# A two-layer decoder trunk: shared early chunks in the mixing's output projection, 512-wide last blocks before a row norm, and residual updates without GpSimd

## The chip, the cores and the metric

The kernel runs on one core of one Trainium2 chip. The metric is the device time of one execution in microseconds (us), as a median of several runs. The engines are named as the profile names them: PE is TensorE, DVE is VectorE, ACT is ScalarE, POOL is GpSimd and SP is SyncE, whose queue issues most of the DMAs.

## The reference

Two layers run over a residual stream of 256 positions and 2048 columns, all in float32. Each layer has three sub-layers, and each sub-layer is normalised before and after:

```python
for l in range(DEPTH):                                   # DEPTH = 2
    xn = rms_norm(h, mix_pre_g[l])
    proj = einsum('bsd,dc->bsc', xn, w_in[l])            # one projection for three head groups
    oa = diff_attention(...)      # 6 heads, 768 columns
    ob = dsa_attention(...)       # 6 heads, 768 columns, top-64 keys by an indexer
    oc = chunk_spatial_gating(gelu(cu), gelu(cv), ...)   # 512 columns
    mix = concatenate([oa, ob, oc], axis=-1)             # 2048 columns
    h = h + rms_norm(mix @ w_out[l], mix_post_g[l])
    xa = memory_attention(rms_norm(h, x_pre_g[l]), rms_norm(mem, mem_g[l]), ...)
    h = h + rms_norm(xa, x_post_g[l])
    ff = swiglu(rms_norm(h, f_pre_g[l]), f_w_gu[l], f_w_down[l])   # hidden width 5632
    h = h + rms_norm(ff, f_post_g[l])
```

`rms_norm(x, g)` divides each row by the root of its mean square and multiplies by `g`.

## The kernel before

**Matmuls and weights.** Every float32 operand is split into a high part `hi` (rounded to the engine's float32r) and a remainder `lo`, and a product is three matmuls: hi by hi, hi by lo, lo by hi. The weights come from memory as 1 MB pieces in three `raw` buffers. ACT makes `hi` (line 206) and DVE makes `lo` (line 207), for 1024 columns at a time, in three buffers each, so up to three split pieces are ready ahead of PE. `plan()` lists the order of all weight pieces. `weights()` hands them out: after each piece's matmuls are written it calls `prefetch` (the next split) and `pump`, which runs what is due (`later`) and lets each waiting generator (`start`) go one step. So the program order of everything beside the matmuls is set by how many weight pieces have gone by. A scheduler then orders each engine's queue by an estimated timeline, except where `ramp` keeps DVE and ACT in the written order.

`mm_t` keeps the weights stationary and streams 256 positions. `mm_n` keeps the 128x128 pieces of the activations stationary (two tiles `t`, positions 0 to 127 and 128 to 255) and streams up to 512 weight columns; with the contraction chunk `k` outside and `t` inside, there are six matmuls for a chunk. Accumulators are four PSUM buffers (`acc`), two for one `mm_n` block.

**The closing projections.** `project_out` (line 648) writes a sub-layer's output in blocks of columns, listed in `TAIL` (line 259): three of 512 and two of 256. It serves the mixing (16 chunks), the cross-attention (4 chunks) and the second half of the feed-forward part (22 chunks, `add=True`: the first half's result is added). After a block ACT squares it with a row sum (`square`, line 550), and it is multiplied by the post-norm gain `gb` into `og`, by DVE (line 673) or, with `add`, by POOL (line 669). The last block's product is put off into `rest` (lines 683 and 681).

**The mixing's first block.** Its 16 chunks come in the order 8 to 11, 0 to 3, 6 and 7, then 4 and 5, then 12 to 15 (`MIX_FIRST`, line 260). Chunks 4 and 5 are the last two heads of the differential attention and 12 to 15 are the gating; both are still computed by generators (`last_heads`, `gating`, `chunks`) while this block runs. The early chunks are read from buffers that the mixing's pool frees later (`early_place`).

**The residual step.** `residual` (line 579) takes the row sums, computes 1/rms (`row_rsqrt`, small DVE instructions at lines 467 to 475), adds `og` times that to the stream `H` (line 604), transposes the new `H` on PE (`turn_x`, line 564) and splits it into the next `x` (lines 212 and 213). After the mixing (`bare` false) the key projection of the memory (`t_k`, stationary weights, moving `mh` and `ml`) covers it, and columns 1024 to 2047 are added by ACT (line 601) and POOL (line 602). Elsewhere (`bare` true) nothing covers it but 38 dummy matmuls (`warm`). The very last step, `last_residual` (line 688), adds some pieces on PE (`hsum`) and the others on DVE, and stores the output.

Of the kernel before, what the change touches and what calls it, by code (L numbers as in the profile page):

```python
# [58 lines left out]
def trunk(ctx: ExitStack, tc, a, onehot, out):  # L59
# [17 lines left out]
    nc.gpsimd.memset(pc.tile([P, 8], F32, name="half_pc"), 0.0)  # L77
# [181 lines left out]
    TAIL = ((0, 512), (512, 512), (1024, 512), (1536, 256), (1792, 256))  # L259
    MIX_FIRST = ((8, 4), (0, 4), (6, 2), (4, 2), (12, 4))  # L260

    def plan():
# [7 lines left out]
        for l in range(L):  # L270
# [25 lines left out]
            for i, (c0, n) in enumerate(TAIL):  # L296
                yield spec(rows(w_out, c0, n), KD, n, MIX_FIRST if i == 0 else None)
# [7 lines left out]
            for hf in range(2):  # L305
# [3 lines left out]
                for c0, n in TAIL:  # L309
                    yield spec(rows(wd, c0, n), nh, n)  # L310
# [88 lines left out]
    def mm_n(nk, cols, xh, xl, hold=False):  # L399

        xh, xl = ([x[:, k, :] for k in range(nk)] if not isinstance(x, list) else x for x in (xh, xl))
        tiles = [acc.tile([P, 512], F32, tag="acc", name="acc") for _ in range(2)]
        for n, k, hi, lo in weights(nk, cols, hold):
            for t in range(2):
                o = tiles[t][:, :cols]
                h, lw = xh[k][:, t * P:(t + 1) * P], xl[k][:, t * P:(t + 1) * P]
                mm(o, h, hi, n == 0, False)
                mm(o, h, lo, False, False)
                mm(o, lw, hi, False, n == nk - 1)
        return tiles  # L410
# [174 lines left out]
    def residual(og, ss, evac, nxt, res, bare, off):  # L585
# [11 lines left out]
        def add(c, n, beside=False):  # L597
            f = slice(c * P, (c + n) * P)
            for t in range(2):
                if beside:  # L600
                    nc.scalar.activation(og[:, t, f], og[:, t, f], AF.Copy, scale=r[:, t:t + 1])
                    nc.gpsimd.tensor_tensor(H[:, t, f], H[:, t, f], og[:, t, f], op=ALU.add)
                else:
                    nc.vector.scalar_tensor_tensor(H[:, t, f], og[:, t, f], r[:, t:t + 1], H[:, t, f],  # L604
                                                   op0=ALU.mult, op1=ALU.add)
# [3 lines left out]


# [6 lines left out]
        if bare:  # L617
            prefetch()
# [6 lines left out]
        add(8, 4, not bare)  # L625
# [4 lines left out]
        add(12, 4, not bare)  # L630
# [17 lines left out]
    def project_out(nk, xh, xl, og, gain, add=False, first=None):  # L648
# [4 lines left out]
        for g, (c0, cols) in enumerate(TAIL):  # L653
# [6 lines left out]
            tiles = mm_n(nk, cols, *(first if first and g == 0 else (xh, xl)), hold=last)  # L660

            def evac(tiles=tiles, g=g, c0=c0, cols=cols, gb=gb, last=last):
# [626 lines left out]
```

## Time and profile before

| what | value |
|---|---|
| median of 3 runs | 2424.31 us (2423.04 to 2426.93) |
| time of the profiled execution | 2425.12 us |
| its span, first to last instruction | 2423.4 us |
| PE busy | 2389.2 us, 99% |
| DVE busy | 1412.6 us, 58% |
| ACT busy | 1188.7 us, 49% |
| POOL busy | 201.9 us, 8% |

Matmuls are pipelined, and the profile models their ends, so "busy" on PE means that one was under way and not that the array ran at its peak. How fast PE runs is better seen from the distance between the starts of neighbouring matmuls. Idle time on DVE, ACT and POOL costs nothing by itself.

### The profile page before, as it was taken

How to read it: one execution, taken by the hardware profiler on the slowest of the kernel's cores; microseconds unless marked ns; L12 is line 12 of the kernel's file. 1: busy time of each engine (PE TensorE's matmuls, PEld its weight loads, DVE VectorE, ACT ScalarE, POOL GpSimd, SP SyncE). 2: the span in 40 equal slices, each digit the busy share in tenths (PEclk: the TensorE clock that was granted, in tenths of full speed). 3: DMA queues.
4: the chain of work that ended last, by engine and by line, in shares of the span. 5: the costliest groups of instructions: out<-in, count | busy, mean ns of one | idle time of the engine just before them, and what ended most of it. 6: DMA issues, size and time to landing. Idle time of an engine off the chain costs nothing.

```text
span 2423.4 us, 42616 instructions
## 1 busy us (share of the span) xinstructions
PE 2389.2 (99%) x17741; PEld 2249.2 (93%) x17741; DVE 1412.6 (58%) x2129; ACT 1188.7 (49%) x1764; POOL 201.9 (8%) x177
## 2 busy tenths in 40 slices
PE   9999999999999999999999999999999999999998
PEld 8899789999998999998999997999999989999987
DVE  5686766665554455555466767666655544555554
ACT  5655545554444444444455655455544444444443
POOL 0010131000000000000100102100000000000001
PEclk9999999999999999999999999999999999999999
DMA  7755475455655565555554555644555555555553
GB/s 250 242 170 157 164 252 176 157 176 196 197 195 194 187 195 193 192 192 192 190 173 132 187 156 189 219 157 157 190 194 192 191 192 190 192 195 196 193 191 131
DMA packets 356757, 453.27 MB, mean 187 GB/s; under 512 B 11290, under 2 KB 275412, under 8 KB 356052
## 3 DMA queue, kind: packets, MB, share of 16 engines
q1 hardware_dynamic: 354836, 443.45, 55.9%
q0 software_dynamic: 1248, 6.29, 0.8%
q8 instruction: 139, 2.28, 0.4%
q10 hardware_dynamic: 480, 0.80, 0.1%
q14 instruction: 54, 0.44, 0.1%
HBM read 444.72 MB, written 5.79 MB: 186 GB/s over the span
## 4 chain that ended last, share of the span: by engine, by line
PE 91%; DVE 4%; ACT 2%; DMA 2%; issue 1%; SPq 0%; POOL 0%; ACTq 0%; POOLq 0%; DVEq 0%
PE acc L201 86%; DVE lo L207 2%; ACT hi L206 1%; PE xtp L564 1%; PE ixp L201 1%; ACT sqj L550 1%; PE lga L201 1%; DMA m<-in_mem_dram 1%; DVE H L604 1%; DMA H<-in_x_dram 0%; DVE mx L207 0%; PE warm L416 0%; DMA lp<-in_a_lambda_dram 0%; PE pvb L201 0%; PE lgx L201 0%
## 5 line engine op out<-in xcount | busy, mean ns | idle before, releaser
L207 DVE TENSOR_TENSOR lo<-raw,hi 128x1024 fp32r<-128x1024 f32 (+2 forms) x839 | 1000.9, 1194 | 870.7 <-ACT hi L206 868.4
L206 ACT ACTIVATE hi<-raw 128x1024 fp32r<-128x1024 f32 (+2 forms) x839 | 861.0, 1027 | 1037.7 <-PE acc L201 954.7
L201 PE MATMUL acc<-x,hi 128*128 128x256 f32 (+1 forms) x7360 | 1270.0, 277 | 0.0
L201 PEld LDWEIGHTS acc<-x,hi 128*128 128x128 f32 (+1 forms) x7360 | 1111.2, 188 | 2.8 <-issue 2.7
L201 PE MATMUL acc<-x,lo 128*128 128x256 f32 x3680 | 889.5, 278 | 6.8 <-DVE lo L207 4.6
L201 PEld LDWEIGHTS acc<-x,lo 128*128 128x128 f32 x3680 | 690.1, 188 | 13.4 <-DVE lo L207 6.1
L201 PE MATMUL acc<-hi,hx 128*128 128x512 f32 (+1 forms) x1760 | 452.6, 347 | 0.0
L201 PEld LDWEIGHTS acc<-hi,hx 128*128 128x128 f32 x1760 | 308.5, 189 | 41.7 <-issue 0.2
L201 PE MATMUL acc<-lo,hx 128*128 128x512 f32 (+1 forms) x880 | 304.9, 347 | 0.0
L201 PEld LDWEIGHTS acc<-lo,hx 128*128 128x128 f32 x880 | 166.7, 189 | 20.5 <-issue 0.2
L1243 POOL TENSOR_TENSOR g<-g,u 128x512 f32<-128x512 f32 x44 | 76.6, 1741 | 1131.3 <-ACT g L1241 1131.3
L201 PE MATMUL acc<-hi,mx 128*128 128x512 f32 (+1 forms) x576 | 148.1, 345 | 7.9 <-DVE mx L207 4.0
L201 PEld LDWEIGHTS acc<-hi,mx 128*128 128x128 f32 x576 | 99.6, 190 | 21.8 <-DVE mx L207 5.1
L201 PE MATMUL acc<-hi,x 128*128 128x384 f32 (+1 forms) x384 | 109.3, 360 | 0.0
L201 PE MATMUL acc<-lo,mx 128*128 128x512 f32 (+1 forms) x288 | 98.4, 343 | 0.1
L201 PEld LDWEIGHTS acc<-hi,x 128*128 128x128 f32 x384 | 70.1, 188 | 8.3 <-issue 3.3
L201 PE MATMUL acc<-lo,x 128*128 128x384 f32 (+1 forms) x192 | 69.7, 363 | 0.0
L212 ACT ACTIVATE x<-xtp,gT 128x256 fp32r<-128x256 f32 x96 | 39.5, 470 | 48.7 <-PE xtp L564 48.7
L201 PEld LDWEIGHTS acc<-lo,mx 128*128 128x128 f32 x288 | 54.6, 190 | 7.0 <-DVE lo L207 1.0
L213 DVE SCALAR_TENSOR_TENSOR x<-xtp,gT,x 128x256 fp32r<-128x256 f32 x96 | 41.6, 478 | 16.1 <-ACT x L212 15.9
L201 PE MATMUL acc<-hi,cx 128*128 128x512 f32 (+1 forms) x160 | 42.7, 352 | 0.0
L201 PEld LDWEIGHTS acc<-lo,x 128*128 128x128 f32 x192 | 36.1, 188 | 3.9 <-issue 1.3
(247 smaller groups left out, 1878.4 us busy)
## 6 DMA issues: line engine op xcount, KB each, us to landing
raw<-in_f_w_gu_dram SPq DMA_DIRECT2D x352, 512.0 KB, 4.5
raw<-in_f_w_down_dram SPq DMA_DIRECT2D x76, 1024.0 KB, 5.1
raw<-in_w_out_dram SPq DMA_DIRECT2D x30, 1024.0 KB, 5.4
raw<-in_w_in_dram SPq DMA_DIRECT2D x48, 512.0 KB, 4.7
raw<-in_w_in_dram SPq DMA_DIRECT2D x23, 1024.0 KB, 5.3
raw<-in_x_wkv_dram SPq DMA_DIRECT2D x16, 1024.0 KB, 4.9
raw<-in_w_in_dram SPq DMA_DIRECT2D x12, 960.0 KB, 5.1
raw<-in_x_wq_dram SPq DMA_DIRECT2D x8, 1024.0 KB, 5.2
```

The source lines that it names most:

```text
L201: return nc.tensor.matmul(o, lhsT=lhsT, rhs=rhs, start=start, stop=stop, skip_group_check=True)
L206: nc.scalar.activation(hi, src, AF.Copy)
L207: eng.tensor_tensor(lo, src, hi.bitcast(F32), op=ALU.subtract)
L212: nc.scalar.activation(hi, src, AF.Copy, scale=scale)
L213: nc.vector.scalar_tensor_tensor(lo, src, scale, hi.bitcast(F32), op0=ALU.mult, op1=ALU.subtract)
L550: nc.scalar.activation(q[:, :src.shape[-1]], src, AF.Square, accum_out=red)
L564: nc.tensor.transpose(p[:, t * P:(t + 1) * P], src[:, t, (c + j) * P:(c + j + 1) * P], ident)
L604: nc.vector.scalar_tensor_tensor(H[:, t, f], og[:, t, f], r[:, t:t + 1], H[:, t, f], op0=ALU.mult, op1=ALU.add)
L1243: nc.gpsimd.tensor_tensor(g, g, u, op=ALU.mult)
```

## The change

The mixing's first two blocks of 512 columns both run their ten early chunks first, into all four accumulators, and then their six late chunks. `TAIL` has four blocks of 512 wherever `project_out` is used; the first feed-forward half keeps the old widths (`HALF`). In a last block the final two chunks run for tile 0 first and then for tile 1, so that tile 0 is complete six matmuls earlier. The residual step after the mixing has an order of its own, two chunks a step, with all updates on DVE; the gain product of a last block is always on DVE. In `last_residual` 24 dummy matmuls are added, and the gain product comes later. Some padding tiles change, which moves the tile `cx` and the work pool by 64 bytes.

```diff
-    nc.gpsimd.memset(pc.tile([P, 8], F32, name="half_pc"), 0.0)
+    nc.gpsimd.memset(pc.tile([P, 24], F32, name="gap"), 0.0)
...
-    TAIL = ((0, 512), (512, 512), (1024, 512), (1536, 256), (1792, 256))
-    MIX_FIRST = ((8, 4), (0, 4), (6, 2), (4, 2), (12, 4))
+    TAIL = ((0, 512), (512, 512), (1024, 512), (1536, 512))
+    HALF = TAIL[:3] + ((1536, 256), (1792, 256))
+    MIX_EARLY, MIX_LATE = ((8, 4), (0, 4), (6, 2)), ((4, 2), (12, 4))
...
-            for i, (c0, n) in enumerate(TAIL):
-                yield spec(rows(w_out, c0, n), KD, n, MIX_FIRST if i == 0 else None)
+            for part, n in ((MIX_EARLY, 10), (MIX_LATE, 6)):
+                for c0, cols in TAIL[:2]:
+                    yield spec(rows(w_out, c0, cols), n, cols, part)
+            for c0, cols in TAIL[2:]:
+                yield spec(rows(w_out, c0, cols), KD, cols)
...
-                for c0, n in TAIL:
+                for c0, n in (HALF, TAIL)[hf]:
                     yield spec(rows(wd, c0, n), nh, n)
...
-    def mm_n(nk, cols, xh, xl, hold=False):
+    def mm_n(nk, cols, xh, xl, hold=False, into=None, more=False):
+        tiles = into or [acc.tile([P, 512], F32, tag="acc", name="acc") for _ in range(2)]
+        def step(t, n, k, hi, lo):
+            o = tiles[t][:, :cols]
+            h, lw = xh[k][:, t * P:(t + 1) * P], xl[k][:, t * P:(t + 1) * P]
+            mm(o, h, hi, n == 0 and not into, False)
+            mm(o, h, lo, False, False)
+            mm(o, lw, hi, False, n == nk - 1 and not more)
+        end = []
+        for w in weights(nk, cols, hold):
+            if hold and w[0] >= nk - 2:
+                end.append(w)
+                if w[0] < nk - 1:
+                    continue
+                for t in range(2):
+                    for w in end:
+                        step(t, *w)
+            else:
+                for t in range(2):
+                    step(t, *w)
...
-        def add(c, n, beside=False):
+        def add(c, n):
             f = slice(c * P, (c + n) * P)
             for t in range(2):
-                if beside:
-                    nc.scalar.activation(og[:, t, f], og[:, t, f], AF.Copy, scale=r[:, t:t + 1])
-                    nc.gpsimd.tensor_tensor(H[:, t, f], H[:, t, f], og[:, t, f], op=ALU.add)
-                else:
-                    nc.vector.scalar_tensor_tensor(H[:, t, f], og[:, t, f], r[:, t:t + 1], H[:, t, f],
-                                                   op0=ALU.mult, op1=ALU.add)
+                nc.vector.scalar_tensor_tensor(H[:, t, f], og[:, t, f], r[:, t:t + 1], H[:, t, f],
+                                               op0=ALU.mult, op1=ALU.add)
...
+        if not bare:
+            add(0, 2)
+            turn(0)
+            add(2, 2)
+            rest()
+            yield
+            turn(2)
+            for c in range(4, KD, 2):
+                add(c, 2)
+                yield
+                turn(c)
+            yield
+            yield from pre_norm(res)
+            return
...
-            tiles = mm_n(nk, cols, *(first if first and g == 0 else (xh, xl)), hold=last)
+            if g < len(early):
+                tiles = mm_n(6, cols, [xh[:, k, :] for k in range(KD)], [xl[:, k, :] for k in range(KD)], into=early[g])
+            else:
+                tiles = mm_n(nk, cols, xh, xl, hold=last)
             def evac(tiles=tiles, g=g, c0=c0, cols=cols, gb=gb, last=last):
+                def scaled(t, eng):
+                    d, p = og[:, t, c0:c0 + cols], tiles[t][:, :cols]
+                    if add:
+                        eng.tensor_tensor(d, d, gb, op=ALU.mult)
+                    else:
+                        nc.vector.tensor_tensor(d, p, gb, op=ALU.mult)
                 for t in range(2):
                     d, p = og[:, t, c0:c0 + cols], tiles[t][:, :cols]
                     if add:
                         nc.vector.tensor_tensor(d, p, d, op=ALU.add)
...
+                    square(d if add else p, ss[:, t, g:g + 1])
+                    if not last:
+                        scaled(t, nc.gpsimd)
+                return lambda: [scaled(t, nc.vector) for t in range(2)]
...
+        warm(24)
         dg = spread(r)
-        rest()
         for t, f in pieces[:3]:
             mm(summed[t, f.start], dg[:, t, :], og[:, t, f], False, True)
         for i in (3, 0, 4, 1, 5, 2, 6, 7):
             t, f = pieces[i]
+            if i == 2:
+                rest()
...
-        at = used[0]
+        at = used[0] + 1
...
+        early = [mm_n(10, cols, *first, more=True) for _, cols in TAIL[:2]]
+        oss, evac = project_out(KD, mxx[:, 0], mxx[:, 1], og, a["mix_post_g"][l], early=early)
...
-        cx = kp.tile([P, 2080], F32R, name="cx")[:, 32:].rearrange("p (a h t) -> p a h t", a=2, h=4)
+        cx = kp.tile([P, 2064], F32R, name="cx")[:, 16:].rearrange("p (a h t) -> p a h t", a=2, h=4)
```

## Rows read from the trace of the kernel before

**Rows 1.** The page: busy time by engine, and the chain that ended last.
```profile
PE 2389.2 (99%) x17741; PEld 2249.2 (93%) x17741; DVE 1412.6 (58%) x2129; ACT 1188.7 (49%) x1764; POOL 201.9 (8%) x177
...
PE 91%; DVE 4%; ACT 2%; DMA 2%; issue 1%; SPq 0%; POOL 0%; ACTq 0%; POOLq 0%; DVEq 0%
```

**Rows 2.** Windows: start:end, length, busy us (instructions) by engine, PE clock, DMA.
```profile
280.00:300.00 20.00, 15.68 (x74) 11.84 (x72) 14.56 (x39) 7.68 (x12) 6.83 (x6) 1.00 0.68 232
...
380.00:400.00 20.00, 17.32 (x138) 17.15 (x137) 16.59 (x24) 15.22 (x36) 5.67 (x4) 0.91 0.42 146
```

**Rows 3.** Waits of PE: total us, times, longest us.
```profile
PE acc L201 <- DVE lo L207: 10.0, 9, 2.7
PE acc L201 <- DVE mx L207: 4.0, 2, 2.0
PE acc L201 <- ACT mx L206: 3.9, 2, 1.9
```

**Rows 4.** Windows over the mixing's first block, and where the clock fell.
```profile
271.00:303.00 32.00, 27.67 (x131) 21.55 (x130) 23.56 (x51) 18.08 (x35) 6.97 (x6) 1.00 0.57 196
387.00:391.00 4.00, 3.77 (x19) 3.80 (x20) 3.92 (x7) 0.62 (x2) 0.00 (x0) 0.57 0.26 88
```

**Rows 5.** Groups of DVE instructions from 271 to 303 us.
```profile
L207 DVE TENSOR_TENSOR lo<-raw,hi 128x1024 fp32r<-128x1024 f32 x8 | 10.8, 1359 | 3.9 <-ACT hi L206 3.7
```

**Rows 6.** Timeline: start, length; H updates beside POOL, PE's wait; the last without POOL.
```profile
378.55 7.40 DVE L604 SCALAR_TENSOR_TENSOR H<-og,rs_r,H 128x256 f32<-128x256 f32 x8
...
379.94 5.73 POOL L602 TENSOR_TENSOR H<-H,og 128x512 f32<-128x512 f32 x4 [3.60 <-ACT og L601]
...
387.23 0.55 PE L201 MATMUL acc<-mh,lo 128*128 128x256 f32 x1 [2.68 <-DVE lo L207]
...
481.59 1.67 DVE L604 SCALAR_TENSOR_TENSOR H<-og,rs_r,H 128x256 f32<-128x256 f32 x4
```

**Rows 7.** Timeline of PE: first and last of four runs of matmuls.
```profile
1173.73 0.84 PE L201 MATMUL acc<-hi,hx 128*128 128x512 f32 x3
...
1178.94 0.39 PE L201 MATMUL acc<-lo,hx 128*128 128x512 f32 x1
...
1203.75 0.40 PE L201 MATMUL acc<-hi,hx 128*128 128x256 f32 x2
...
1210.59 0.40 PE L201 MATMUL acc<-hi,hx 128*128 128x256 f32 x2
...
468.79 0.39 PE L201 MATMUL acc<-lo,cx 128*128 128x512 f32 x1
...
472.29 0.39 PE L201 MATMUL acc<-lo,cx 128*128 128x512 f32 x1
...
473.00 0.39 PE L201 MATMUL acc<-hi,cx 128*128 128x256 f32 x2
...
474.02 0.50 PE L201 MATMUL acc<-hi,cx 128*128 128x256 f32 x3
```

**Rows 8.** Groups by form: count, busy us, mean ns of one.
```profile
L207 DVE TENSOR_TENSOR lo<-raw,hi 128x1024 fp32r<-128x1024 f32 x759 | 936.8, 1235 | 830.4 <-ACT hi L206 828.3
...
L213 DVE SCALAR_TENSOR_TENSOR x<-xtp,gT,x 128x256 fp32r<-128x256 f32 x96 | 41.6, 478 | 16.1 <-ACT x L212 15.9
...
L550 ACT ACTIVATE sqj<-acc 128x512 f32<-128x512 f32 x24 | 14.2, 590 | 14.0 <-PE acc L201 13.8
...
L673 DVE TENSOR_TENSOR og<-acc,gb 128x512 f32<-128x512 f32 x12 | 8.2, 683 | 1.4 <-ACT sqj L550 1.4
...
L550 ACT ACTIVATE sqj<-acc 128x256 f32<-128x256 f32 x16 | 6.1, 379 | 7.0 <-PE acc L201 7.0
```

**Rows 9.** Timeline of the kernel's end: DVE, PE and ACT.
```profile
2412.00 0.74 DVE L467 TENSOR_SCALAR rs_v<-ssr 128x2 f32<-128x2 f32 x1
...
2414.92 4.34 PE L201 MATMUL hsum<-og,dg 128*128 128x512 f32 x6 [2.68 <-DVE dg L487]
...
2419.30 0.60 ACT L706 ACTIVATE H<-hsum 128x512 f32<-128x512 f32 x1 [0.26 <-PE hsum L201]
```

More of the change, by code (lines that the diff above doesn't have):

```diff
@@ L397, in mm_t @@
         return tiles
-    def mm_n(nk, cols, xh, xl, hold=False):
+    def mm_n(nk, cols, xh, xl, hold=False, into=None, more=False):
         xh, xl = ([x[:, k, :] for k in range(nk)] if not isinstance(x, list) else x for x in (xh, xl))
[L402 to L409, printed above, removed]
+        tiles = into or [acc.tile([P, 512], F32, tag="acc", name="acc") for _ in range(2)]
[17 more added lines that the diff above has]
+                    step(t, *w)
         return tiles
@@ L616, in residual @@
         add(4, 2)
-        if bare:
-            prefetch()
+        prefetch()
         rest()
@@ L624, in residual @@
         turn(6)
-        add(8, 4, not bare)
+        add(8, 4)
         yield
@@ L629, in residual @@
         turn(10)
-        add(12, 4, not bare)
+        add(12, 4)
         yield
@@ L646, in begin, with project_out @@
         start(gen)
-    def project_out(nk, xh, xl, og, gain, add=False, first=None):
+    def project_out(nk, xh, xl, og, gain, add=False, early=()):
         ss = sm.tile([P, 2, len(TAIL)], F32, tag="sso", name="sso", bufs=2)
@@ L666, in evac @@
                         nc.vector.tensor_tensor(d, p, d, op=ALU.add)
-                        square(d, ss[:, t, g:g + 1])
-                        if not last:
-                            nc.gpsimd.tensor_tensor(d, d, gb, op=ALU.mult)
-                    else:
-                        square(p, ss[:, t, g:g + 1])
-                        if not last:
-                            nc.vector.tensor_tensor(d, p, gb, op=ALU.mult)
-                if not last:
-                    return
-                def rest():
-                    for t in range(2):
-                        d, p = og[:, t, c0:c0 + cols], tiles[t][:, :cols]
-                        if add:
-                            nc.gpsimd.tensor_tensor(d, d, gb, op=ALU.mult)
-                        else:
-                            nc.vector.tensor_tensor(d, p, gb, op=ALU.mult)
-                return rest
+                    square(d if add else p, ss[:, t, g:g + 1])
+                    if not last:
+                        scaled(t, nc.gpsimd)
+                return lambda: [scaled(t, nc.vector) for t in range(2)]
             if last:
@@ L1120, in trunk @@
         pool = {}
-        at = used[0]
+        at = used[0] + 1
         def turn_memory():
-            while used[0] == at or any(g.__name__ in ("last_heads", "chunks") for g in side):
+            while used[0] <= at or any(g.__name__ in ("last_heads", "chunks") for g in side):
                 yield
@@ L1132, in trunk @@
         start(turn_memory())
-        oss, evac = project_out(KD, mxx[:, 0], mxx[:, 1], og, a["mix_post_g"][l], first=first)
+        early = [mm_n(10, cols, *first, more=True) for _, cols in TAIL[:2]]
+        oss, evac = project_out(KD, mxx[:, 0], mxx[:, 1], og, a["mix_post_g"][l], early=early)
         kp = pool["kp"]
@@ L1250, in trunk @@
             if hf == 0:
-                for c0, cols in TAIL:
+                for c0, cols in HALF:
                     t_d = mm_n(nh, cols, hh, hl)
```

## The prediction

> **What bounds the kernel now.** I read the page first. PE is busy for 2389 of 2423 us, and the chain that ended last is PE's for 91% [rows 1]: time can only come from PE's remaining waits, from slow matmuls, or from the ends where nothing follows. I then cut the span into windows of 20 us. The feed-forward windows are full. The dents in each layer are the mixing's closing (15.68 of 20 us busy) and the stretch after it, where the next key projection runs beside the residual step: 17.32 busy, at a mean clock of 0.91 [rows 2]. Layer 1 repeats both with nearly the same numbers. PE's waits say what ends them: twice 2.0 us for DVE's and twice 1.9 us for ACT's split of a late mixing chunk, and 2.7 us for a weight split, the longest of nine [rows 3]. Last I compared starts of neighbouring matmuls, form by form, since "busy" hides their rate.
>
> The reader is to see two different illnesses. In the closing, DVE is busy for only 23.56 of 32 us while PE waits [rows 4]: the data are late because their chain is long, and matmuls that could run are queued behind those that cannot. In the key projection DVE is the late engine itself. Eight updates of `H` take 7.40 us beside four POOL additions of 5.73 us together, where four without POOL take 1.67 [rows 6]; so eight should take 3.34, and 4.06 us are lost. The weight split queues behind them, PE waits 2.68 us [rows 6], and then the clock is at half: 0.57 over 387 to 391 [rows 4].
>
> **The change part by part.** The sum is made against the profiled execution, 2425.12 us.
>
> *Shared early chunks.* The second block's ten early chunks now stand where PE waited: 60 matmuls of 0.2265 us (from 1173.73 to 1178.94 there are 23 starts [rows 7]), 13.6 us more cover. Chunks 4 and 5 arrived 2 us late and 12 to 15 about 2 us late behind them, so 13.6 us covers both, unless DVE falls behind. Over the twenty early chunks (27.2 us of PE) it has ten weight splits of 1.235 us [rows 8], 12.4 us, and what it does now beside splits, 23.56 less 10.8 [rows 4, 5], 12.8 us: 25.2 in all. Tight, but four of the eight chunk splits are wanted only by the third block. Now 7.9 us are lost over both layers [rows 3]; I leave 0.4 a layer: **-7.1** (bounds -7.9 and 0). The second block now reads 60 of its matmuls from early copies, whose address may suit PE less; by the slower 512-wide row, 0.2333 [rows 7], that is 0.4 us a layer at most: **+0.4** (0 to 0.8). The accumulators: block one and two hold all four until block one's late chunks end. Its emptying (two squares of 0.59, two products of 0.683 [rows 8]) hides under block two's 36 late matmuls, 8.2 us; without that cover it would cost 2.5. Loads keep their bytes; one more is issued on SP. `turn_memory` starts after 20 chunks and not 16, some 60 us before the key projection needs it: nothing. POOL issues four gain loads and not five.
>
> *Updates without ACT and POOL.* DVE now does sixteen updates of 0.42 (1.67/4 [rows 6]), 6.7 us; sixteen chunk splits of 0.478 [rows 8], 7.6; two gain products of 0.683, 1.4; the 1/rms chain, 2.9 (2412.00 to 2414.92 [rows 9], an upper value); eight weight splits, 9.9. That is 28.5 us against a key projection of 192 narrow matmuls at 0.1133 (473.00 to 474.02 is nine [rows 7]), 21.8 us, plus PE's own transposes. The surplus runs into the query projection, which wants a further chunk only every 12 x 0.1133 = 1.36 us. What matters is order: updates now come two chunks at a time, so a weight split stands behind some 1.8 us of DVE work and not behind 7.40, and up to two split pieces are ready beyond the one in use. Nothing else queues on POOL here. Gone would be the waits (2.7 a layer) and the half clock: 4 us at 0.57 is 1.7 us, of which some is the wait itself, so 1.5. I leave 0.5 a layer: **-7.4** (bounds -8.4 and 0).
>
> *Blocks of 512.* In the mixing and the feed-forward part a pair of 256-wide matmuls takes 0.240 us (1203.75 to 1210.59 is 57 starts) and one of 512 takes 0.2265 [rows 7]. Pairs that go: 16 x 6 = 96 and 22 x 6 = 132 a layer, 456 in all, at 13.5 ns: -6.2. In the cross-attention it is the other way: 0.2333 for 512 and 0.1133 for 256 [rows 7], so 48 pairs cost +0.3, unless the 64 bytes by which `cx` moves change its rate; at 0.2265 throughout it would be -1.0. Together **-5.9** (-7.2 to -5.9).
>
> The Trainium skill, "TensorE: Matmul & The Clock Gate", section "Back-to-back issue gap", gives the distance of warm matmuls as columns / 2.4 + 2.5 ns. By it one of 512 saves only 2.6 ns over two of 256, and this term would be an estimated -1.3. I go by the rows, since block three beside the narrow ones has the same operands.
>
> *Three row norms with only dummy matmuls as cover.* The wide last block makes the square 0.59 long and not 0.38 [rows 8], and the sum before it longer alike. But tile 0 is complete six matmuls, 1.36 us, earlier, so its share is done when tile 1 ends. Two gain products on DVE, 1.4 us, enter the ramp, where DVE has gaps while it waits for PE's transposes; uncovered they would delay the next split by 1.4. POOL no longer stands beside the chain (a 0.17 us instruction took 0.74 beside it at the end [rows 9]). I take **0** (-0.6 to +0.7 each).
>
> *The end.* The 24 dummies fill PE's 2.68 us wait, so the six `hsum` matmuls (4.34 us, partly at half clock [rows 9]) may run at full clock, about 1.5 us sooner. Then DVE ends last: five 0.68 us pieces from 2414.69 end at 2418.1, and two products more make 2419.5, against 2419.90 for the last ACT copy. The chain loses the 0.57 us beside POOL. **-0.9** (-1.8 to 0).
>
> Sum: -7.1 + 0.4 - 7.4 - 5.9 + 0 - 0.9 = -20.9; 2425.12 - 20.9 = 2404.2. The profiled execution is 0.8 above the median of the three runs, so **2403.4** as a median.
>
> **The rivals.**
>
> *The key projection keeps its wait.* DVE's 28.5 us exceed PE's time there, and the scheduler may still put updates and chunk splits in a row. For: it did so before, eight in a row. Against: 4.06 us of those were POOL's doing. Price: the 7.4 come back, 2411.
>
> *The closing still waits.* Twenty early chunks load DVE to 25.2 of 27.2 us, so the late chunks may come later than they do now. For half of the wait to stay costs 3.6: 2407.
>
> *The width buys nothing.* The narrow rate may belong to where `hi` and `lo` lie and not to the width; `cx` shows the opposite order [rows 7]. If one of 512 saves only a tenth or two of the 13.5 ns, the term falls to about -1: 2408.
>
> By the formula of the Trainium skill ("TensorE: Matmul & The Clock Gate", "Back-to-back issue gap") it would also be an estimated 2408.
>
> *Moved tiles.* If the padding doesn't keep the addresses of the mixing's and feed-forward pools, 7 x 132 wide matmuls a layer may run at 0.2333: 1848 x 6.8 ns = 12.6 us, and 528 narrow ones gain 3.5: 2412.
>
> *The other side: DVE serves its own work before the weight splits, in closing and key projection.* Now it does so once a layer. At the extreme all 12.8 us in the closing and all 18.6 (28.5 - 9.9) in the key projection go first; less the 5.4 us that two ready pieces cover (24 matmuls), PE waits 7.4 and 13.2 us, each with 1.5 for the clock. Over what I leave, that is 22.6 a layer, 45.2 in all: 2449. It decides the sign once more than 57% of it happens (25.8 us to reach 2429.2); at three quarters the time is 2437. Against it: splits are written ahead of each step, and they were slipped into the 1/rms chain before.
>
> **How the numbers follow.** The forecast's case, with its bounds (2397 to 2407), has 0.60; the key projection's wait 0.14; the closing's 0.08; the width 0.05; moved tiles 0.05; the slow side 0.04; better than 2397 0.04. Low end: nearly all waits and the end's whole 1.8 us, 2395. High end: both waits kept in part, 2414. A measurement of this kernel tells about 0.2%, 4.8 us, from no change. All cases but the slow one end faster by more than that; with some weight for two of them together, and for a schedule that moves work elsewhere, faster is 0.90, same 0.05, slower 0.05. The likeliest time is 2403.
>
> **What would show it.** Right: no wait for `mx` on PE between the gating projection and the third block; starts 0.2265 apart in all four blocks; no half clock after the mixing; updates of 0.42 us each in pairs, no POOL beside them; `hsum` at full clock. Wrong: a wait for `lo` over 2 us in the key projection, with the clock at half after it; PE waiting for a transpose whose update is late; the third block waiting for an accumulator; a last block at 0.233. The prediction fails as a whole if DVE is more than 90% busy over both stretches and PE waits there for its weight splits.

## The result, and the profile after

The kernel after takes 2398.47 us (median of 4 runs, 2397.03 to 2399.35), the kernel before 2424.39 beside it: a ratio of 0.9891, 95% interval 0.9874 to 0.9908. The forecast was 2403 us, with a range of 2395 to 2414. The profiled execution is the one of 2399.35 us, 25.8 below that of before. The page of after, busy time by engine and the chain that ended last (before: [rows 1]):

```profile
PE 2379.1 (99%) x17261; PEld 2224.6 (93%) x17261; DVE 1406.9 (59%) x2131; ACT 1183.4 (49%) x1726; POOL 184.0 (8%) x159
...
PE 95%; ACT 2%; DVE 2%; DMA 1%; issue 0%; SPq 0%; POOL 0%; ACTq 0%; POOLq 0%; DVEq 0%
```

PE is the chain even more than before. The largest sum among its waits (total us, times, longest; before: [rows 3]), and the windows over the closing's early part and over the key projection, with busy us of each engine and then the clock (before: [rows 2, 4]):

```profile
PE acc L201 <- DVE lo L207: 4.3, 7, 0.8
```

```profile
272.00:300.00 28.00, 28.00 (x133) 23.26 (x132) 21.22 (x48) 18.02 (x34) 3.98 (x2) 1.00 0.53 170
366.00:391.00 25.00, 25.00 (x217) 24.94 (x216) 23.59 (x61) 18.58 (x38) 0.54 (x1) 1.00 0.49 180
```

No wait for `mx` is left, and none for `lo` over 0.8 us. Both dents are full, at full clock: 28.00 of 28.00 and 25.00 of 25.00 us. DVE is at 94% in the second (23.59 of 25.00 us), so it has little to spare there.

Where the time went is read from starts of matmuls in PE's timeline, stretch by stretch. This table is worked out from them (us; layer 0, layer 1; the last column is after less before, both layers):

| stretch | before | after | change | forecast |
|---|---|---|---|---|
| start of the span to the closing of layer 0 | 271.26 | 272.20 | +0.9 | 0 |
| closing, first matmul on an early copy to the mixing's last | 101.14, 97.17 | 93.81, 90.46 | -14.0 | -9.3 |
| from there to the query projection's first | 29.50, 29.46 | 25.14, 25.14 | -8.7 | -7.4 |
| cross-attention's closing | 23.86, 23.86 | 23.31, 23.31 | -1.1 | +0.3 |
| second feed-forward closing | 121.33, 122.17 | 119.47, 121.24 | -2.8 | -3.6 |
| three row norms with dummies, in order of time | 5.74, 7.08, 5.74 | 5.85, 6.29, 5.85 | -0.6 | 0 |
| last closing matmul to the span's end | 13.15 | 13.52 | +0.4 | -0.9 |

The sum is -25.9, against -25.7 by the spans; the rest of the kernel is as it was. (The forecast's -2.6 and -3.6 for the width stand in the lines where the pairs are.) The first line is no part of the change: over all kernels below the closing of layer 0 starts between 270.6 and 274.6 us after the span's start, and PE's wait for the first pieces of `x`, 0.2 to 2.8 us, varies with it. So spans are compared from there on.

### The profile page after: what moved, and what is told of

The parts are those of the page before. It is cut to its first block, busy times and chain, and to the rows that moved or that the text cites. A ratio compares the mean times of both kernels' runs of the same rounds, so it can differ in the third digit from the quotient of the medians.

```text
span 2397.7 us, 41589 instructions
## 1 busy us (share of the span) xinstructions
PE 2379.1 (99%) x17261; PEld 2224.6 (93%) x17261; DVE 1406.9 (59%) x2131; ACT 1183.4 (49%) x1726; POOL 184.0 (8%) x159
## 3 DMA queue, kind: packets, MB, share of 16 engines
q0 software_dynamic: 1216, 6.29, 0.8%
## 4 chain that ended last, share of the span: by engine, by line
PE 95%; ACT 2%; DVE 2%; DMA 1%; issue 0%; SPq 0%; POOL 0%; ACTq 0%; POOLq 0%; DVEq 0%
PE acc L201 89%; PE xtp L584 1%; DVE lo L207 1%; PE ixp L201 1%; ACT sqj L570 1%; ACT hi L206 1%; PE lga L201 1%; PE warm L436 1%; DMA m<-in_mem_dram 1%; PE pva L201 0%; PE pvb L201 0%; PE ptp L444 0%; PE lgx L201 0%; PE pvx L201 0%; ACT x L212 0%
## 5 line engine op out<-in xcount | busy, mean ns | idle before, releaser
L207 DVE TENSOR_TENSOR lo<-raw,hi 128x1024 fp32r<-128x1024 f32 (+3 forms) x833 | 1000.9, 1203 | 869.0 <-ACT hi L206 866.7
L206 ACT ACTIVATE hi<-raw 128x1024 fp32r<-128x1024 f32 (+3 forms) x833 | 859.9, 1033 | 1026.9 <-PE acc L201 947.2
L201 PEld LDWEIGHTS acc<-hi,hx 128*128 128x128 f32 x1584 | 286.4, 189 | 48.4 <-issue 0.2
L201 PEld LDWEIGHTS acc<-lo,hx 128*128 128x128 f32 x792 | 149.4, 189 | 23.9 <-issue 0.2
L201 PE MATMUL acc<-hi,mx 128*128 128x512 f32 x384 | 120.7, 391 | 0.0
L201 PEld LDWEIGHTS acc<-hi,mx 128*128 128x128 f32 x384 | 71.9, 188 | 14.8 <-DVE mx L207 0.2
L201 PE MATMUL acc<-lo,mx 128*128 128x512 f32 x192 | 75.0, 391 | 0.0
L201 PEld LDWEIGHTS acc<-lo,mx 128*128 128x128 f32 x192 | 36.1, 188 | 7.4
L201 PE MATMUL acc<-hi,m 128*128 128x512 f32 x128 | 41.8, 398 | 0.0
L201 PE MATMUL acc<-hi,cx 128*128 128x512 f32 x128 | 41.2, 395 | 0.0
```

Source lines behind the costliest of these rows:

```text
L201: return nc.tensor.matmul(o, lhsT=lhsT, rhs=rhs, start=start, stop=stop, skip_group_check=True)
L206: nc.scalar.activation(hi, src, AF.Copy)
L207: eng.tensor_tensor(lo, src, hi.bitcast(F32), op=ALU.subtract)
```

## The experiments

**The shared early chunks alone**, on the kernel before:

```
-            tiles = mm_n(nk, cols, *(first if first and g == 0 else (xh, xl)), hold=last)
+            if g < len(early):
+                tiles = mm_n(6, cols, ..., into=early[g])
...
+        early = [mm_n(10, cols, *first, more=True) for _, cols in TAIL[:2]]
```

> The kernel before with the shared early chunks alone (five blocks, updates with ACT and POOL as before). Cover theory: the waits and short gaps of the closing go by the longer cover alone; from the first matmul that reads an early copy to the last of the mixing it took 101.1 us in layer 0 and 97.2 in layer 1 before, and 93.8 and 90.5 after with 1.3 of that from the width. So about 95.1 and 91.8 here, the key projection as before with its wait and its half clock, and about 2413 us in all. Rival, the term as I priced it (6.7 us for both layers): 96.8 and 93.8... and 2417.5. Rival, the cover works only together with the other two parts, or the key projection pays it back: over 2420.

Measured: 2414.07 us, ratio 0.9944 (0.9930 to 0.9958). Its closing takes 95.95 and 91.88 us, 5.2 and 5.3 less than before: 10.5 in all. Windows of it, closing and key projection:

```profile
275.00:303.00 28.00, 28.00 (x136) 23.34 (x135) 21.52 (x49) 17.68 (x32) 3.98 (x2) 1.00 0.51 169
371.00:400.00 29.00, 26.30 (x216) 26.12 (x216) 24.45 (x49) 20.50 (x44) 6.29 (x5) 0.94 0.46 155
```

The closing's window is full without the other two parts. The key projection keeps its 2.7 us wait in both layers; the lower clock comes behind it in layer 0 alone (29.6 us at a mean of 0.94; 28.1 us in layer 1, at 1.00). The cover works by itself, and is worth half as much again as I had priced it.

**A shorter cover**: the kernel after, with four early chunks of the second block in place of ten.

```
-            for part, n in ((MIX_EARLY, 10), (MIX_LATE, 6)):
+            for part in (MIX_EARLY, MIX_EARLY[:1], MIX_LATE, MIX_EARLY[1:] + MIX_LATE):
...
-        early = [mm_n(10, cols, *first, more=True) for _, cols in TAIL[:2]]
+        early = [mm_n(n, cols, *first, more=True) for n, (_, cols) in zip((10, 4), TAIL[:2])]
```

> The kernel after with only four of the second block's chunks early and not ten: 14 early chunks, 24 matmuls or 5.4 us of cover more than before, and not 60 or 13.6. Threshold theory: what was late came about 2 us late twice, so 5.4 us is nearly enough: the closing within 1 us of the kernel after in each layer (93.8 and 90.5), 2398.5 to 2400.5 in all. Rival, it is DVE's sum of work and the gain grows with the cover: 40% of it, some 3 us a layer lost again, 2404 to 2405.

Measured: 2403.98 us, ratio 0.9908 (0.9894 to 0.9921). The closing takes 97.63 and 92.59 us, 3.8 and 2.1 more than in the kernel after. So four chunks of ten give some 4.5 of the 10.5 us (10.5 less 5.95), and my threshold theory, which left at most 1 us a layer, falls. That the gain grows evenly with the cover isn't shown either: what is lost is one wait a layer, and in layer 0 the clock behind it. PE waits for a weight split that took 2.07 us where one takes 1.235 [rows 8], and POOL multiplies beside it (timeline of POOL, DVE and PE, in brackets the idle time ahead and what ended it; then windows of the 4 us from the wait on, layer 0 and layer 1, the clock third from the end):

```profile
296.95 3.49 POOL L1117 TENSOR_TENSOR MX<-MX,y 128x512 f32<-128x512 f32 x2 [5.58 <-DVE y L1115]
...
297.24 2.07 DVE L207 TENSOR_TENSOR lo<-raw,hi 128x1024 fp32r<-128x1024 f32 x1
...
299.37 0.76 PE L201 MATMUL acc<-lo,mx 128*128 128x512 f32 x1 [1.52 <-DVE lo L207]
```

```profile
299.00:303.00 4.00, 3.63 (x9) 2.88 (x10) 2.68 (x3) 0.63 (x1) 2.09 (x3) 0.57 0.98 321
1491.00:1495.00 4.00, 3.79 (x17) 3.14 (x18) 3.02 (x4) 1.69 (x2) 3.67 (x5) 1.00 0.97 355
```

The wait is 1.52 us in both layers; at the clock of 0.57 layer 0 loses an estimated 1.7 us more (4 us times 0.43), which is the difference between 3.8 and 2.1.

**The updates: POOL or order?** Four kernels have the update step in four mixtures. First, the kernel before with all updates on DVE, in its old order of four chunks at a time:

```
-        add(8, 4, not bare)
+        add(8, 4)
...
-        add(12, 4, not bare)
+        add(12, 4)
```

> The kernel before, its sixteen residual updates after the mixing all on DVE, still written four chunks at a time. Engine theory (POOL and ACT beside DVE made the updates long): the stretch from the last matmul of the mixing to the first of the query projection falls from 29.5 to about 25.1 us in both layers, no half clock there, about 2415.7 us in all. Order theory (what counts is that weight splits are not queued behind a long row of updates, as my prediction had it): eight updates of 0.42 us still stand together, some 3.3 us, and four more than before are DVE's; the stretch stays over 27.5 us and the whole over 2420.

Then the kernel after, with ACT and POOL back for columns from 1024 on, in the new order:

```
         def add(c, n):
             f = slice(c * P, (c + n) * P)
             for t in range(2):
+                if c >= 8 and not bare:
+                    nc.scalar.activation(og[:, t, f], og[:, t, f], AF.Copy, scale=r[:, t:t + 1])
+                    nc.gpsimd.tensor_tensor(H[:, t, f], H[:, t, f], og[:, t, f], op=ALU.add)
+                else:
```

> The kernel after, with ACT's scaling and POOL's addition back for columns from 1024 on after the mixing, written two chunks at a time as in the new order. Engine theory: updates beside POOL are twice as long again, the stretch from the last matmul of the mixing to the query projection goes back to 28 to 29.5 us, with a wait for a weight split of about 2 us; 2405 to 2407 us. Order theory: the new order keeps the splits ahead, the stretch stays at 25 to 26 us; 2398 to 2400.

Then the kernel after with the old step whole:

```
-            for c in range(4, KD, 2):
-                add(c, 2)
-                yield
-                turn(c)
...
+        add(8, 4, not bare)
...
+        add(12, 4, not bare)
```

> The kernel after with the whole residual step of before after the mixing: four chunks at a time, columns from 1024 on by ACT and POOL in pieces of 512. With the updates on DVE alone the wait went in the old order too, and with POOL in the new order most of it went as well (25.1 to 26.5 us for the stretch from the last matmul of the mixing to the first of the query projection, in place of 29.5). If the two are remedies of one wait, either of them enough, here with neither the stretch is 29 to 29.5 us again and the whole about 2406. Rival: other parts of the change (wide last block, earlier memory) already shortened it, and the updates count little: 26 to 27 us, 2401.

Measured: 2416.26 us (0.9957, 0.9944 to 0.9969) for the first; 2401.46 (0.9895, 0.9881 to 0.9908) for the second; 2407.11 (0.9922, 0.9908 to 0.9936) for the third. From the mixing's last matmul to the query projection they take 24.99 and 24.75 us; 26.53 and 26.49; 29.82 and 28.18. So POOL's absence is enough in the old order, the new step recovers most with POOL in place, and with neither the wait is back, 2.4 us long (with the lower clock behind it in layer 0 alone, as above). Neither of my two theories alone predicts all three. What goes with the wait in all of them is how long DVE's row of updates lasts before its next weight split. Timeline rows of it (start, length, count): after; the first; the second (with POOL's row); the third.

```profile
372.16 4.44 DVE L620 SCALAR_TENSOR_TENSOR H<-og,rs_r,H 128x256 f32<-128x256 f32 x11
```

```profile
381.16 3.26 DVE L604 SCALAR_TENSOR_TENSOR H<-og,rs_r,H 128x256 f32<-128x256 f32 x8
```

```profile
371.70 5.22 DVE L624 SCALAR_TENSOR_TENSOR H<-og,rs_r,H 128x256 f32<-128x256 f32 x8
...
373.18 8.41 POOL L622 TENSOR_TENSOR H<-H,og 128x256 f32<-128x256 f32 x8 [4.82 <-ACT og L621]
...
376.85 3.44 DVE L207 TENSOR_TENSOR lo<-raw,hi 128x1024 fp32r<-128x1024 f32 x2
```

```profile
372.54 6.42 DVE L624 SCALAR_TENSOR_TENSOR H<-og,rs_r,H 128x256 f32<-128x256 f32 x8
...
374.24 5.86 POOL L622 TENSOR_TENSOR H<-H,og 128x512 f32<-128x512 f32 x4 [5.03 <-ACT og L621]
...
381.32 0.50 PE L201 MATMUL acc<-mh,lo 128*128 128x256 f32 x1 [2.38 <-DVE lo L207]
```

Rows of 3.26 and 4.44 us leave PE no wait; 5.22, with two slow splits behind, leaves 0.7, 6.42 leaves 2.4, and the 7.40 of before [rows 6] 2.7. POOL works through the length of one update (0.65 to 0.93 us beside it as a mean of the row, 0.41 without), and of the splits too (1.72 beside it, 1.235 without). It is POOL and not ACT: in the kernel after, updates with ACT at work through most of their time take 0.48 us each, as the others do. The second and the third mixture differ in one more thing than order: POOL adds in pieces of 256 columns in the second and of 512 in the third. An update that lies wholly beside such an addition takes 0.97 us in the second and 1.5 in the third and before. So how much of what the second recovers is due to the order, and how much to POOL's shorter pieces, isn't shown. The updates do not come two chunks at a time in any kernel; the scheduler puts 8 or 11 in a row, and 15 in the next kernel.

**Five closing blocks again**, in the kernel after:

```
-    TAIL = ((0, 512), (512, 512), (1024, 512), (1536, 512))
-    HALF = TAIL[:3] + ((1536, 256), (1792, 256))
+    TAIL = ((0, 512), (512, 512), (1024, 512), (1536, 256), (1792, 256))
+    HALF = TAIL
```

> The kernel after with five closing blocks again (the last two of 256 columns) in mixing, cross-attention and both feed-forward halves; padding set so that the later tiles lie as in the kernel after. Width theory: 96 and 132 pairs of matmuls a layer at 13.5 ns are 6.2 us, those of the cross-attention nothing (0.2265 for 512, 0.1133 for 256 with cx where it lies now); the row norm's ramps change by up to 0.8 each: 2404.5 us (2403 to 2406). Rival, the gain came with the moved tiles and not with the width: within 1 us of the kernel after, 2398 to 2400.

Measured: 2406.22 us, ratio 0.9912 (0.9898 to 0.9925), a span 6.4 longer: +3.6 in the two mixing closings, +2.8 in the two feed-forward ones, +0.8 in the cross-attention, +1.1 over key and query projection (here 15 updates stand in a row, 6.03 us, with waits of 0.7), -1.0 at the end. That is just above my range. In the mixing's +3.6 a wait of 0.7 for the memory's DMA in layer 0 is contained, which the kernel after doesn't have. So in the mixing and the feed-forward part the width is worth about what the rows of before said, and the scheduler's row of updates hangs on it as well. In the cross-attention I had the narrow rate wrong. Two rows of its 256-wide closing matmuls, 45 starts apart:

```profile
464.02 0.28 PE L201 MATMUL acc<-lo,cx 128*128 128x256 f32 x1
...
469.42 0.28 PE L201 MATMUL acc<-lo,cx 128*128 128x256 f32 x1
```

That is 0.120 us a matmul (5.40 over 45) where `cx` lies now, and it was 0.1133 where it lay before [rows 7].

**cx where it lay before:**

```
-        cx = kp.tile([P, 2064], F32R, name="cx")[:, 16:]...
+        cx = kp.tile([P, 2080], F32R, name="cx")[:, 32:]...
```

> The kernel after with cx 64 bytes further, where it lay before. Address theory: its 512-wide matmuls start 0.2333 us apart again and not 0.227, the cross-attention's closing is 23.9 us and not 23.3, in both layers. Rival, the rate came with the width: 0.227 and 23.3 as in the kernel after.

Measured (one run, 2402.59 us), from PE's timeline: 23.88 us in both layers, about as before (23.86), against 23.31 in the kernel after. Two rows of it near the closing's end, five matmuls apart, and two of the kernel after, nine apart:

```profile
468.68 0.39 PE L201 MATMUL acc<-hi,cx 128*128 128x512 f32 x1
...
469.85 0.40 PE L201 MATMUL acc<-hi,cx 128*128 128x512 f32 x1
```

```profile
464.82 0.39 PE L201 MATMUL acc<-lo,cx 128*128 128x512 f32 x1
...
466.86 0.40 PE L201 MATMUL acc<-hi,cx 128*128 128x512 f32 x1
```

That is 0.234 us a matmul here (1.17 over five) and 0.227 there (2.04 over nine), at one width. The 64 bytes made that rate. They move the two widths in opposite ways: 0.2333 and 0.1133 for 512 and 256 columns at the old place, 0.227 and 0.120 at the new one, and there `cx` has the rates of `hx` (0.2265 and 0.120 [rows 7]). So one matmul of 512 saves some 13 ns over two of 256 at the new place, and costs 6.7 more than two at the old one: what a wide block is worth hangs on where the activations lie.

**Four blocks in the first feed-forward half too:**

```
-    HALF = TAIL[:3] + ((1536, 256), (1792, 256))
+    HALF = TAIL
```

> The kernel after with four closing blocks of 512 in the first feed-forward half too. In layer 0 the second half's closing went from 121.3 to 119.5 us by it, so 1.8 us a layer: 3.6 us, about 2395. Rival, the first half has no row norm behind it but ACT's evacuation and the next gating matmuls that wait for the accumulators: what is won waits there, 2398.

Measured: 2414.12 us, ratio 0.9949 (0.9936 to 0.9961). Neither theory: some 15 us slower than the kernel after. The closing does save 1.9 us a layer; but the gating projection behind it takes 248.6 us and not 239.3, in both layers, and no wait shows. Window of 200 us inside it, here and in the kernel after:

```profile
850.00:1050.00 200.00, 200.00 (x1700) 200.00 (x1699) 103.58 (x98) 84.71 (x89) 15.81 (x9) 1.00 0.57 187
```

```profile
850.00:1050.00 200.00, 200.00 (x1767) 200.00 (x1767) 106.53 (x101) 88.02 (x92) 15.84 (x9) 1.00 0.60 195
```

Both are 200.00 us busy at a clock of 1.00; one starts a matmul every 117.6 ns, the other every 113.2. The operands are the same. "Busy" shows nothing of it; only the count does. Next, the same kernel with four dummy matmuls in between:

```
                     later(d_out)
+                warm(4)
             else:
```

> The kernel with four closing blocks of 512 in both feed-forward halves, and four dummy matmuls of 256 columns between the last closing block of the first half and the gating projection behind it. Without them each of that projection's 2112 matmuls started 117.7 ns after the one before and not 113.3, in both layers, 9.4 us a layer, with the same operands at the same places. Mode theory: the slow spacing is a state that PE keeps when matmuls of 256 with the weights stationary follow a stream of 512 without a break (in the key projection behind the mixing it is there too, and ends at the first transposes); the dummies break it: 113.3 again, 239.3 us for the projection, 0.5 us for the dummies, 2395 to 2396 in all. Rival, it is where the weight buffers stand in their rotation, which one load fewer shifts: 117.7 and 248.6 us as without dummies, 2414.

Measured: 2398.29 us, ratio 0.9882 (0.9867 to 0.9896). The projection is back at 239.3 us, in both layers:

```profile
850.00:1050.00 200.00, 200.00 (x1767) 200.00 (x1767) 106.54 (x101) 87.91 (x92) 15.85 (x9) 1.00 0.60 195
```

The rotation of the weight buffers is the one of the slow kernel, so it isn't the cause. From the last `hx` matmul of 512 straight into the projection the slow spacing stays for 2112 matmuls, and with 0.5 us of other matmuls ahead it doesn't come. The total is above the 2395 to 2396 that I expected; from the closing of layer 0 on the trace is 2.2 us shorter than that of the kernel after (2123.3 against 2125.4), of 2.5 by the blocks. That the 512-wide stream is the cause, as my mode theory has it, is shown for this place only: the last section has the slow spacing beginning elsewhere.

**The end.** The three `hsum` matmuls on `H` (two instructions each) kept behind the last block, and DVE's and ACT's instructions in the order written:

```
-            mm(p, ident, H[:, t, f], True, False)
-        warm(24)
+            tc.keep_in_program_order(mm(p, ident, H[:, t, f], True, False))
+        warm(20)
...
-            last_residual(og, oss, evac)
+            with tc.manual_schedule(engines={DVE, ACT}):
+                last_residual(og, oss, evac)
```

> The kernel after with the three hsum matmuls on H kept behind the last closing block, 20 dummies in place of 24, and the last residual's DVE and ACT instructions in the order written, so that the two gain products stand behind the 1/rms chain. Theory of the end (from the last closing matmul on, the span is the chain up to the first store and then 8.0 us of stores): the block is 1.55 us shorter, the chain 0.6; the span 2.1 us less, 2396. Rival, the copies from PSUM are what ends last, and the hsum matmuls now stand in front of them: no less than after.

Measured: 2398.26 us, ratio 0.9885 (0.9869 to 0.9902); by the trace the last closing takes 119.47 us and not 121.24, and the end behind it 13.47 and not 13.52: the block gave 1.8 us, the chain next to nothing of its 0.6. Then the kernel after with most of the output not stored:

```
             if p is not None:
                 nc.scalar.activation(H[:, t, f], p, AF.Copy)
...
+            if i not in (3, 0, 7):
+                continue
             (nc.sync if p is None else nc.scalar).dma_start(out[0, t * P:(t + 1) * P, f], H[:, t, f])
```

> The kernel after with five of the eight output pieces not stored (so five eighths of the output are missing): only the first of DVE's, the first of ACT's copies and the last of DVE's are. Store theory: in the kernel after 2 MB of stores leave together at some 340 GB/s and end 5.1 us behind the last compute; with three eighths of them the end comes 2.5 to 3.5 us sooner. Rival, the end is a fixed latency behind the last store issued: within 0.5 us of 5.1 behind the last compute as in the kernel after.

Measured (one run, 2398.95 us): from the last closing matmul to the end 11.1 us, 2.4 less than with eight pieces, and 2.7 us behind the last compute where it was 5.1. So the number of stores moves the end. Timeline rows of before (stores' issue); of the kernel after (chain, copies, stores' issue) with two windows behind them (DMA share and GB/s last); of the kernel with three stores (its last copies); and of the kernel with `hsum` kept behind:

```profile
2415.46 2.98 SPq L710 DMA_DIRECT2D out_dram<-H  x5
```

```profile
2386.11 0.16 DVE L575 TENSOR_REDUCE ssr<-sso 128x2 f32<-128x8 f32 x1 [0.25 <-ACT sqj L570]
2386.19 0.68 DVE L698 TENSOR_TENSOR og<-og,gF 128x512 f32<-128x512 f32 x1
2386.79 0.16 DVE L487 TENSOR_SCALAR rs_v<-ssr 128x2 f32<-128x2 f32 x1
...
2389.13 2.81 PE L201 MATMUL hsum<-og,dg 128*128 128x512 f32 x6 [0.88 <-DVE dg L507]
...
2389.67 3.12 SPq L737 DMA_DIRECT2D out_dram<-H  x5
...
2391.34 1.24 ACT L733 ACTIVATE H<-hsum 128x512 f32<-128x512 f32 x2 [0.47 <-PE hsum L201]
```

```profile
2390.00:2394.00 4.00, 1.94 (x5) 0.57 (x3) 2.29 (x4) 1.79 (x3) 0.00 (x0) 1.00 0.87 329
2391.00:2396.00 5.00, 0.94 (x3) 0.11 (x1) 1.29 (x2) 1.20 (x2) 0.00 (x0) 0.83 1.01 380
```

```profile
2393.26 1.26 ACT L733 ACTIVATE H<-hsum 128x512 f32<-128x512 f32 x2 [0.45 <-PE hsum L201]
```

```profile
2383.98 0.16 DVE L575 TENSOR_REDUCE ssr<-sso 128x2 f32<-128x8 f32 x1 [0.85 <-ACT sqj L570]
2384.18 0.17 DVE L487 TENSOR_SCALAR rs_v<-ssr 128x2 f32<-128x2 f32 x1
...
2387.07 4.18 SPq L737 DMA_DIRECT2D out_dram<-H  x5
...
2387.21 2.74 PE L201 MATMUL hsum<-og,dg 128*128 128x512 f32 x6
...
2391.00 0.60 ACT L733 ACTIVATE H<-hsum 128x512 f32<-128x512 f32 x1 [0.41 <-ACT H L733]
```

From 2391 to 2396 the DMA engines are busy throughout (share 1.01), at 380 GB/s. In the kernel after a gain product stands between `ssr` and `rs_v`, 0.5 us of the chain. Without it the first store is issued 5.06 us behind the last closing matmul (2382.01) and not 5.54 (2384.13). But from there to the end it is now 8.4 us and not 8.0. The last copy from PSUM ends 9.6 us behind the last closing matmul (2391.60) and not 8.45 (2392.58); in front of the copies now stand the 20 dummies and six `hsum` matmuls more, so the rival is right in part.

**Both gains together**, with 14 dummies at the end:

> The kernel after with both of what the last runs gave: four closing blocks of 512 and four dummy matmuls in the first feed-forward half, and the hsum matmuls on H behind the last closing block, with 14 dummies and the gain products behind the 1/rms chain. If the two are independent, 2 x 1.27 us from the blocks and 1.9 to 2.3 from the end: a span of about 2393 where the x of the start comes as early as in the kernel after, 0.987 of before. Rival, the timing of one stage again depends on what stands ahead of it: a stretch at 117.7 ns or an end no earlier, 2396 to 2400.

Measured: 2394.36 us, ratio 0.9874 (0.9858 to 0.9891), a span of 2391.5. Its interval overlaps that of the kernel after, so the times alone don't part the two; from the closing of layer 0 to the end the trace has 2120.8 us here and 2125.4 there (spans of 2391.52 and 2397.65 less 270.76 and 272.21), 4.7 less where 2.5 and 1.9 to 2.3 were added up. It is the fastest of all kernels here.

## Why the prediction was right, and where it was not

**Shared early chunks: mechanism right, term too small.** I put -7.1 and +0.4; alone it measures -10.5, outside my bounds. The term that was mis-sized is the loss: I took it from PE's waits, 7.9 us. That view counts idle time behind a modelled end, and short gaps don't appear in it. Three neighbours in the closing of before, with no wait beside them:

```profile
295.83 0.71 PE L201 MATMUL acc<-hi,mx 128*128 128x512 f32 x2
296.58 0.50 PE L201 MATMUL acc<-lo,mx 128*128 128x512 f32 x1
296.92 0.39 PE L201 MATMUL acc<-hi,mx 128*128 128x512 f32 x1
```

Two matmuls take 0.75 us and one 0.34 where 0.45 and 0.227 would do. The 2.6 us beyond the waits were not added up gap by gap. The 0.4 a layer that I left did not stay either. That the closing still waits, a rival, was wrong; with four chunks in place of ten one wait of 1.5 us a layer is left, and nothing between was tried.

One reading was wrong as well. I took the closing's data as late "because their chain is long" and saw POOL's doing in the key projection alone. Rows of the closing before (POOL; DVE's two splits; the wait that they end):

```profile
287.69 3.78 POOL L1079 TENSOR_TENSOR vg<-vg,lnb 128x512 f32<-128x512 f32 x2 [122.60 <-ACT MX L1015]
...
288.04 2.31 DVE L207 TENSOR_TENSOR lo<-raw,hi 128x1024 fp32r<-128x1024 f32 x1
...
290.27 1.74 DVE L207 TENSOR_TENSOR mx<-MX,mx 128x512 fp32r<-128x512 f32 x1
...
292.07 0.97 PE L201 MATMUL acc<-hi,mx 128*128 128x512 f32 x3 [2.04 <-DVE mx L207]
```

A weight split takes 1.235 us otherwise [rows 8], and the `mx` split 0.68 in the kernel after. So beside POOL's product the two are some 2.1 us longer, as much as the whole wait for DVE's split of a chunk, and layer 1 repeats it. The other wait of the closing, for ACT's split, is not of this kind. The longer cover hides such a stretch (in the kernel after one weight split still takes 2.23 us beside that product); the closing before without POOL's product there was not tried. POOL does not stretch every split beside it: beside its `mh` products all splits of the kernel before stay at 1.21 to 1.23 us.

**Updates: sum near, reason half right.** -7.4 against -8.7, just past my bound of -8.4; the wait and the half clock are both gone, as forecast, and the 0.5 a layer that I left with them. POOL stretches updates and splits, as I read it. "What matters is order: updates now come two chunks at a time" is the step that failed: they don't. What holds without POOL is that a row of updates ahead of a weight split costs nothing at 4.4 us and 0.7 at 6.0; this fits the 5.4 us that the slow rival gave two ready pieces. The stretch takes 25.14 us here and 24.99 and 24.75 in the first mixture, whose last block is 256 wide: behind the 512-wide one the first 77 matmuls start 117.8 ns apart and not 113.3, an estimated 0.35 us a layer.

**Width: right where tiles stayed.** 132 pairs in the second feed-forward half of layer 0 gave 1.86 us, 14.1 ns a pair, where I had 13.5. By the Trainium skill's formula ("TensorE: Matmul & The Clock Gate", section "Back-to-back issue gap"), which that section gives for a single matmul and not for a stream with its weight loads, it would be an estimated 2.5 ns a pair (the prediction has 2.6); this trace doesn't bear that out, and the rival by it falls. In layer 1 half of the gain went into `hsum` matmuls that the scheduler put into the block. In the cross-attention I took +0.3 and named -1.0 as the bound if `cx` changes its rate by moving; that bound came true, -1.1, and the run with `cx` back shows the place to be the cause. Of the rival that the narrow rate belongs to a place and not to the width this much is right: for `cx`, 64 bytes turn the order of the two widths round. `hx`, `hi` and `lo` were not moved. "Moved tiles" as I priced it didn't happen.

**Row norms.** -0.6 lies within the bounds. The one between the layers became 0.8 us shorter; it isn't the width, since with five blocks it is 6.29 us as well. What else did it was not tried.

**The end: wrong sign.** -0.9 forecast; +0.4 behind the last matmul, and 0.9 of the width's gain lost ahead of it. The dummies did bring full clock: six `hsum` matmuls take 2.81 us where they took 4.34 [rows 9]. And the last compute ends 1.2 us sooner, about as the term has it: 8.45 us behind the last closing matmul (2392.58) where it was 9.66 (2419.90 [rows 9]). The failed step is that DVE or ACT ends last. The stores do: the end comes 3.5 us behind the last compute before and 5.1 after, but 7.9 and 8.0 us behind the first store. And the first store waits for the 1/rms chain, not for `hsum`.

**The slow side** did not come. Its beginning is seen where the scheduler makes a row long: 15 updates before a split in the kernel with five blocks, at 0.7 us a layer.

**The total.** Against the forecast the lines of the table are off by -8.0 us (closing, key projection, cross-attention, row norms) and by +3.0 (start, feed-forward closing, end). Two terms lie past their bounds. Without the errors that cancel, the total would stand at the low edge of the range, some 2396 us; that it stands clear of it is luck.

## What to carry to other kernels

A wait's size is read from starts of neighbours, not from a view of waits alone: the closing's loss was a third larger than its waits. A helper engine can slow the late engine by more than it takes over (here one update from 0.48 to 1.5 us), and in more than one stage; what counts is how long the row of work is that stands ahead of the instruction that the critical path wants. Whoever changes one stage compares the matmul spacing, as a count per window, in the stages behind it: the largest effect found here, 9.4 us a layer, lay in a stage that nobody touched and that was 100% busy either way.

## What the runs showed of the hardware

Matmuls of 256 columns with the weights stationary have two spacings at the same clock, with the same operands: 113.3 and 117.7 ns. Directly behind a stream of 512-wide matmuls it was the slow one wherever a kernel here has that sequence, and it stayed until something else ran. The kernel after has it in its own key projection (timeline: first and sixty-first matmul behind the mixing, and two starts 36 matmuls apart behind the first transposes):

```profile
366.24 0.28 PE L201 MATMUL acc<-mh,lo 128*128 128x256 f32 x1
...
373.31 0.28 PE L201 MATMUL acc<-mh,lo 128*128 128x256 f32 x1
...
378.39 0.28 PE L201 MATMUL acc<-mh,lo 128*128 128x256 f32 x1
...
382.48 0.28 PE L201 MATMUL acc<-mh,lo 128*128 128x256 f32 x1
```

7.07 us over 60 matmuls are 117.8 ns, 4.09 over 36 are 113.6. That the first half's last two blocks are narrow hides this in the kernel after: from narrow `hx` matmuls the projection goes on at 113.3.

But the 512-wide stream is not the only way into the slow spacing, and an interruption does not always end it. In the kernel after, one stream of the layer-0 gating projection goes on after a wait of 0.77 us, with no 512-wide matmul near:

```profile
500.04 0.28 PE L201 MATMUL acc<-x,hi 128*128 128x256 f32 x1
...
503.10 0.28 PE L201 MATMUL acc<-x,lo 128*128 128x256 f32 x1
...
504.71 0.38 PE L201 MATMUL acc<-x,lo 128*128 128x256 f32 x1 [0.77 <-DVE lo L207]
...
505.17 0.28 PE L201 MATMUL acc<-x,hi 128*128 128x256 f32 x1
...
510.47 0.28 PE L201 MATMUL acc<-x,lo 128*128 128x256 f32 x1
```

3.06 us over 27 starts ahead of the wait are 113.3 ns, 5.30 over 45 behind it are 117.8. In the kernel before, 41 starts from 497.30 to 502.12, behind transposes, are 117.6 ns apart. So an interruption can bring either spacing; the four dummies brought the fast one in both layers, in both kernels that have them. What PE does differently in the two and what chooses between them is not settled, nor whether the 64 bytes of `cx` choose between the same two states.
